# Gate and up of a SwiGLU layer on TensorE: the right operands of the quarter-block products are made step by step between units, and are used from the second and the third pair on

## The chip, the core and the metric

The kernel runs on one core of one Trainium2 chip. The metric is the device time of one execution in microseconds; the time of a kernel is the median over several runs. A profile of one execution shows every instruction of the engines: TensorE (PE, with its weight loads PEld), VectorE (DVE), ScalarE (ACT), GpSimd (POOL) and SyncE (SP), whose queue issues most of the DMA transfers.

## What is computed

One encoder layer on 1024 tokens of width 1024. After the mixers and the first norm, the feed-forward part is the stretch that matters here (cut from the reference):

```
g = jnp.einsum('bsd,df->bsf', h, w_ffn_gate[i])
up = jnp.einsum('bsd,df->bsf', h, w_ffn_up[i])
ffn = jnp.einsum('bsf,fd->bsd', jax.nn.silu(g) * up, w_ffn_down[i])
ple = jnp.einsum('bsr,rd->bsd', p[i], w_ple_proj[i])
ple_gate = jax.nn.sigmoid(jnp.einsum('bsd,de->bse', h, w_ple_gate[i]))
h = _layer_norm(ALPHA * h + ffn + ple_gate * ple, ln2_gain[i], ln2_bias[i])
```

The hidden width is 2816, which is 22 blocks of 128, taken as 11 pairs of blocks.

## The kernel before

**Precision.** Each fp32 operand is split in a high part (an ACT copy to a rounded type, L71) and a low part (a DVE subtraction, L72), both in `split` (L70). A product of two operands is three matmuls, high by high, high by low and low by high: `mm3c` with L783, L784 and L785.

**Gate and up.** Per pair of hidden blocks, gate and up are a 2 by 2 block product in the Strassen-Winograd form with seven products, numbered 1 to 7. The left operands are weights and sums of weights, the right operands (`RIGHT`, one per product) are halves of the transposed hidden state and sums of them, made once ahead of the stage. Each product has two units, m = 0 for gate and m = 1 for up; a unit is 12 matmuls of 128x128 by 128x512. A pair without finer products has the units 1, 1, 2, 2, 6, 6, 7, 7, 5, 5, 4, 4, 3, 3 (`plan`, L1420).

**Finer products.** The products 2 and 4 can themselves be done in seven quarter-block products over gate and up together (`FINE`, L1164). They take 42 matmuls of 128x256 in four parts f0 to f3 (`f_unit`, L1409; `mm_fine`, L1278) in place of 24 of 128x512, and the parts stand between the units of other products: 1, 1, f0, 6, f1, 6, f2, 7, f3, 7 for product 2, and f0, 5, f1, 5, f2, 3, f3, 3 for product 4. They need four further right operands of product 2 and four of product 4, sums of quarter blocks of the hidden state. `fine_right` (L1182) makes them with `make` (L1193): for each of two row blocks three DVE sums of 128x256 (L1197, L1198, L1199), an ACT copy and a DVE subtraction (`split`), all in one scratch tile `fs`. `FROM` (L1165) says from which pair each product is done finely.

**Order.** PE, DVE, ACT, POOL and SP run the program in the order in which the code issues it. All five are queues in order. The loop over the units k (L1779 on) issues the matmuls of unit k, then its `post` (what reads the result out of PSUM), then one of the eight calls of `make` if k is in a list (L1782), and then, in `ahead_g` (L1733), work for later units out of the list `items`. An item is a unit number, a duration that the writer estimated and a function; it is taken while the estimated room of the present unit lasts, up to nine units ahead, or at once if its unit is next.

**Who waits for whom.** The products 1, 6 and 7 of one m are added up in one PSUM bank (`bmm`), and ACT copies the running sum out between them: L1360 after product 1, L1362 after product 6, L1367 after product 7 (`post`, L1344). So the matmuls of product 7 wait for the copy after product 6, and that copy stands on ACT behind whatever splits were issued earlier. The parts of a fine product share banks likewise (`bo` for product 2, `bs` for product 4): f1 waits for the DVE addition that reads f0 out (L1304 in `post_fine`, L1293), f3 for the one after f2. DVE additions that read out products 2, 3 and 5 are L1353, the product of the two halves of 4 is L1376, and L1326 and L1330 finish a pair.

**Down.** Behind the last unit the down product starts with four banks; `dsets` (L1681) names them: the first set is `s` (banks `bs`), then `t` (banks `bmm`; the names were exchanged in L775).

Below, **pair 0** is the first of the 11 pairs, and a unit (6,0) is product 6 with m = 0.

Of the kernel before, what the change touches and what calls it, by code (L numbers as in the profile page):

```python
# [42 lines left out]
def layer(tc, xT, xn, w_first, w_mt, w_rv, w_out, w_pg, w_pe, pT, w_gu, w_dn,  # L43
# [1118 lines left out]

    Q = HF // 2
    FINE = ((1, 5, 2), (6,), (7,), (4, 3))  # L1164
    FROM = {2: 2, 4: 3}  # L1165
    oslots = []
    frights, fsum = {}, []
    TAGS = {0: "t", 1: "o", 2: "mm", 4: "s"}
# [13 lines left out]
    def fine_right(p, places):  # L1182

        R = RIGHT[p]

        def blk(i, j, part):
            return R[:, part, 2 * i:2 * i + 2, j * Q:(j + 1) * Q]

        f = frights[p] = {q: (blk(*ij, 0), blk(*ij, 1)) for q, ij in {1: (0, 0), 2: (1, 0), 3: (1, 1)}.items()}
        f.update(zip((7, 5, 6), places))  # L1190
        f[4] = blk(0, 1, 0), blk(0, 1, 1)

        def make(q, left, right):  # L1193
            x = fsum[3]
            for kt in range(2):
                (lh, ll), (rh, rl) = ([v[:, kt, :].bitcast(F32) for v in side] for side in (left, right))
                dve.tensor_tensor(x, lh, rh, ALU.subtract)  # L1197
                dve.tensor_tensor(x, x, ll, ALU.add)  # L1198
                dve.tensor_tensor(x, x, rl, ALU.subtract)  # L1199
                split(x, *(v[:, kt, :] for v in f[q]))  # L1200

        b = lambda i, j: (blk(i, j, 0), blk(i, j, 1))
        return [lambda: make(7, b(1, 1), b(0, 1)), lambda: make(5, b(0, 1), b(0, 0)),
                lambda: make(6, b(1, 1), f[5]), lambda: make(4, b(1, 0), f[6])]

    stores = []

    class Pair:
# [32 lines left out]
        def prep_fine(self, p, part):  # L1241

            f = self.fine[p]

            def xy():
                return [self.raw[m, p == 4, 1] for m in range(2)]

            def sums():
                x, y = xy()
                dve.tensor_tensor(fsum[0], y[:, :Q], y[:, Q:], ALU.add)  # L1250
                dve.tensor_tensor(fsum[1], fsum[0], x[:, :Q], ALU.subtract)
                dve.tensor_tensor(fsum[2], x[:, :Q], y[:, :Q], ALU.subtract)
# [425 lines left out]

    seq = [(1, 0), (5, 0), (2, 0), (3, 0), (6, 0), (1, 1), (7, 0), (2, 1), (4, 0), (5, 1), (6, 1), (3, 1), (7, 1), (4, 1)]
    which = {(0, 0): 0, (0, 1): 1, (0, 2): 0, (1, 0): 1, (1, 1): 1, (1, 2): 0}  # L1680
    dsets = (("s", "t"), ("o", "mm"))  # L1681
    dunits = []

    def d_units(p, s):
# [81 lines left out]
    with tc.manual_schedule(engines={ET.PE, ET.DVE, ET.Activation, ET.Pool, ET.SP}):  # L1766
# [126 lines left out]
```

## Time and profile before

| what | value |
|---|---|
| median of three runs | 1188.23 us (1187.18 to 1189.41) |
| profiled execution, its own time | 1188.74 us |
| its span, first to last instruction | 1187.0 us |
| PE busy | 1167.6 us, 98% of the span |
| DVE busy | 894.8 us, 75% |
| ACT busy | 578.6 us, 49% |
| gate and up, from the first matmul to the first of down | 539.96 to 968.40 us |

A row of the timeline gives the start from the start of the span, the duration, the engine, the line of the kernel, the operation, the tile written and those read, the shape, and in brackets how long the engine was idle ahead of it and what ended that. A matmul's duration runs to its modelled end, and the next begins before that, so the pace is read from the starts. The table by stretches gives busy time per engine in each stretch, and the granted clock of PE as a share of full speed.

### The profile page before, as it was taken

Reading aid. Unit: us, or ns where it says so; the run is one execution under the profiler, and the core shown is the slowest. Engines: PE = TensorE matmul, PEld = TensorE weight load, DVE = VectorE, ACT = ScalarE, POOL = GpSimd, SP = SyncE. Lnnn points to the kernel's source line nnn. Section 1 sums busy time; section 2 is a strip of 40 time slices with the busy share of each in tenths; the row PEclk is TensorE's granted clock in tenths of the full one; section 3 lists DMA queues with packets and bytes.
Section 4 is the critical chain, followed back from the end, with each engine's and each line's share of the span. In section 5 each row is a group of like instructions: output and inputs, shape, how many; then the busy total and the mean of one; then the engine's idle time right before and its main releaser. Section 6 shows DMA issues by size and latency. Waiting matters only on the chain.

```text
span 1187.0 us, 17890 instructions
## 1 busy us (share of the span) xinstructions
PE 1167.6 (98%) x6374; PEld 981.0 (83%) x6374; DVE 894.8 (75%) x1732; ACT 578.6 (49%) x1177; POOL 119.3 (10%) x181
## 2 busy tenths in 40 slices
PE   9999999999999999999989999999999999999997
PEld 7888888888888888888867888888888888888885
DVE  5565777766759788957878788888888886774677
ACT  5666348676756265123344344433444345552463
POOL 2001011202010130000000000000000011124242
PEclk9999999999999999999989999999999999999999
DMA  7345656555346955665223232322323289999977
GB/s 254 104 160 215 238 171 238 182 168 186 127 172 244 359 179 207 235 219 173 81 70 133 83 113 72 133 98 99 131 74 117 87 241 340 346 236 222 256 166 206
DMA packets 80665, 211.76 MB, mean 178 GB/s; under 512 B 9536, under 2 KB 14784, under 8 KB 80576
## 3 DMA queue, kind: packets, MB, share of 16 engines
q1 hardware_dynamic: 71936, 193.84, 46.2%
q0 software_dynamic: 8640, 16.78, 8.0%
q8 instruction: 50, 0.82, 0.3%
q14 instruction: 39, 0.32, 0.1%
HBM read 139.29 MB, written 62.13 MB: 170 GB/s over the span
## 4 chain that ended last, share of the span: by engine, by line
PE 83%; DVE 9%; ACT 4%; issue 2%; DMA 1%; SPq 0%; DVEq 0%; POOL 0%; ACTq 0%; POOLq 0%
PE bmm L783 7%; PE bmm L784 7%; PE bmm L785 7%; PE bmm L77 5%; PE bmm L79 5%; PE bmm L78 5%; PE bt L783 5%; PE bt L784 5%; PE bt L785 5%; PE bs L783 4%; PE bs L785 4%; PE bs L784 4%; PE bo L783 3%; PE bo L785 3%; PE bo L784 3%
## 5 line engine op out<-in xcount | busy, mean ns | idle before, releaser
L77 PE MATMUL bmm<-H,w 128*128 128x512 f32 x240 | 97.4, 406 | 0.0
L79 PE MATMUL bmm<-H,w 128*128 128x512 f32 x240 | 94.2, 393 | 0.0
L78 PE MATMUL bmm<-H,w 128*128 128x512 f32 x240 | 94.1, 392 | 0.0
L1500 POOL DMA_DIRECT2D h0b<-in_w_dn x24 | 21.6, 900 | 553.6 <-PE bt L785 518.5
L1324 ACT ACTIVATE ev<-ev 128x512 f32<-128x512 f32 x41 | 25.9, 633 | 89.8 <-DVE ev L1353 71.4
L72 DVE TENSOR_TENSOR w<-raw,w 128x512 fp32r<-128x512 f32 (+1 forms) x61 | 39.6, 658 | 18.9 <-ACT w L71 18.7
L77 PEld LDWEIGHTS bmm<-H,w 128*128 128x128 f32 x240 | 45.3, 189 | 9.8 <-ACT H L71 0.7
L79 PEld LDWEIGHTS bmm<-H,w 128*128 128x128 f32 x240 | 45.1, 188 | 9.9
L78 PEld LDWEIGHTS bmm<-H,w 128*128 128x128 f32 x240 | 45.2, 189 | 7.7
L535 ACT ACTIVATE sc<-sc,st 128x385 f32<-128x385 f32 (+1 forms) x64 | 37.1, 584 | 16.8 <-DVE st L533 16.7
L71 ACT ACTIVATE w<-raw 128x512 fp32r<-128x512 f32 (+1 forms) x61 | 35.8, 597 | 17.4 <-PE bo L79 7.6
L531 DVE CUSTOM_DVE_ANT_0 sc<-cst,bs,skb 128x384 f32<-128x384 f32 (+1 forms) x64 | 34.9, 576 | 8.9 <-PE bs L530 7.8
L783 PE MATMUL bmm<-H,u 128*128 128x512 f32 x88 | 35.8, 407 | 3.4 <-ACT ev L1362 3.4
L783 PE MATMUL bmm<-H,w 128*128 128x512 f32 x88 | 35.2, 400 | 3.9 <-ACT ev L1360 2.4
L1326 DVE TENSOR_TENSOR ev<-ev 128x512 f32<-128x512 f32 x41 | 28.4, 692 | 12.8 <-ACT ev L1324 11.9
L784 PE MATMUL bmm<-H,u 128*128 128x512 f32 x88 | 35.5, 403 | 0.0
L785 PE MATMUL bmm<-H,u 128*128 128x512 f32 x88 | 35.3, 401 | 0.0
L1353 DVE TENSOR_TENSOR ev<-ev,bt 128x512 f32<-128x512 f32 x44 | 30.0, 682 | 6.7 <-PE bt L785 6.7
L784 PE MATMUL bmm<-H,w 128*128 128x512 f32 x88 | 35.0, 398 | 0.0
L785 PE MATMUL bmm<-H,w 128*128 128x512 f32 x88 | 35.0, 398 | 0.0
L541 ACT ACTIVATE sc<-sc,st 128x384 f32<-128x384 f32 (+1 forms) x64 | 34.0, 579 | 0.8 <-DVE st L539 0.8
L71 ACT ACTIVATE H<-ln 128x512 fp32r<-128x512 f32 (+1 forms) x34 | 22.9, 677 | 21.5 <-DVE ln L1032 7.2
(786 smaller groups left out, 3845.1 us busy)
## 6 DMA issues: line engine op xcount, KB each, us to landing
ad<-ev SPq DMA_DIRECT2D x33, 512.0 KB, 3.4
pgd<-pro SPq DMA_DIRECT2D x28, 512.0 KB, 2.9
raw<-in_w_gu SPq DMA_DIRECT2D x22, 512.0 KB, 3.6
ln<-in_w_gu SPq DMA_DIRECT2D x22, 512.0 KB, 4.1
raw<-ad SPq DMA_DIRECT2D x40, 256.0 KB, 6.0
ln<-ad SPq DMA_DIRECT2D x37, 256.0 KB, 6.0
H<-in_w_dn SPq DMA_DIRECT2D x33, 256.0 KB, 6.6
wod<-aq SPq DMA_DIRECT2D x15, 512.0 KB, 2.7
```

The source lines that it names most:

```text
L71: act.activation(hi, raw, AF.Copy)
L72: dve.tensor_tensor(lo, raw, hi.bitcast(F32), ALU.subtract)
L77: pe.matmul(o, lh, rh, start=start, stop=False)
L78: pe.matmul(o, lh, rl, start=False, stop=False)
L79: recent[0] = pe.matmul(o, ll, rh, start=False, stop=stop).ins.name
L531: dve.tensor_tensor_reduce(sc[g][:, :nk], cst[:, tc0:tc0 + nk], b[:, :nk], slope(i, g), skb[:, 2 * i + g:2 * i + g + 1], ALU.add, ALU.max, ...
L535: act.activation(sc[g][:, :nk + 1], sc[g][:, :nk + 1], AF.Exp, bias=st_[:, 1, j, g:g + 1], accum_out=st_[:, 2, j, g:g + 1])
L541: behind(act.activation(sc[g][:, :nk], sc[g][:, :nk], AF.Copy, scale=st_[:, 3, j, g:g + 1]))
L783: pe.matmul(o, lh, rh, start=start, stop=False, skip_group_check=True)
L784: pe.matmul(o, lh, rl, start=False, stop=False, skip_group_check=True)
L785: pe.matmul(o, ll, rh, start=False, stop=stop, skip_group_check=True)
L1353: dve.tensor_tensor(get(name), ev[left][:, m, :], right, ALU.add)
```

## The change

Product 2 is done finely from pair 1 on (it was pair 2), product 4 from pair 2 on (it was pair 3). The eight makes are enqueued after the units 2, 4, 7, 9 of pair 0 and 20, 23, 26, 28 of pair 1 (it was 5, 8, 14, 18, 21, 24, 27 and 42, in the old count of units). A make is no longer issued in one piece: it is a list of steps that are put into `items`, one between every two of the items that are there. Six of the eight (all of product 2, and the operands 7 and 5 of product 4) work on both row blocks at once, as 128x(2x256), in a scratch tile `fwide` of their own; the other two work on a row block at a time as before, in `fs`. `last` uses `fsum[1]` in place of that scratch. The first set of banks of the down product is `t`, then `s`.

```
-    FROM = {2: 2, 4: 3}
+    FROM = {2: 1, 4: 2}
...
         def make(q, left, right):
-            x = fsum[3]
-            for kt in range(2):
-                (lh, ll), (rh, rl) = ([v[:, kt, :].bitcast(F32) for v in side] for side in (left, right))
-                dve.tensor_tensor(x, lh, rh, ALU.subtract)
-                dve.tensor_tensor(x, x, ll, ALU.add)
-                dve.tensor_tensor(x, x, rl, ALU.subtract)
-                split(x, *(v[:, kt, :] for v in f[q]))
+            def steps(x, c, us):
+                def rows(pair):
+                    return [v[:, c, :].bitcast(F32) for v in pair]
+
+                return [(us, lambda: dve.tensor_tensor(x, rows(left)[0], rows(right or f[6])[0], ALU.subtract)),
+                        (us, lambda: dve.tensor_tensor(x, x, rows(left)[1], ALU.add)),
+                        (us, lambda: dve.tensor_tensor(x, x, rows(right or f[6])[1], ALU.subtract)),
+                        (us, lambda: split(x, *(v[:, c, :] for v in f[q])))]
+
+            if p == 2 or q in (7, 5):
+                return steps(fwide, slice(0, 2), 0.62)
+            return steps(fsum[3], 0, 0.36) + steps(fsum[3], 1, 0.36)
...
-    dsets = (("s", "t"), ("o", "mm"))
+    dsets = (("t", "s"), ("o", "mm"))
...
+        FINE4 = len(plan(0)) + len(plan(1)) - 2
+        FINES = (2, 4, 7, 9, 20, 23, 26, FINE4)
         ahead_g(-1, 4)
         for k in range(NG):
             gunits[k][1]()
             gunits[k][2]()
-            if k in (5, 8, 14, 18, 21, 24, 27) or k == FINE4:
-                fine.pop(0)()
-                debt[0] += 2.6
+            if k in FINES:
+                if len(fine) == 2:
+                    frights[4][6] = tuple(ct([P, 2, Q], "p", 2, F32R) for _ in range(2))
+                at = max([-1] + [i for i, x in enumerate(items) if x[4:]]) + 1
+                for i, x in enumerate(fine.pop(0)):
+                    at += at > 0
+                    items.insert(at, (items[at][0], 0, *x, True))
+                    at += 1
```

**DVE in pair 0, around the read-out of product 5 (rows into `ev_5333` from `bt`).** Before, a whole make of eight DVE instructions (L1197 to L1199 and the low part, L72, twice) stands between the read-outs of (5,0) and (5,1):

```order
L72 TENSOR_TENSOR u_5324<-raw_5421,u_5324 128x512
L1353 TENSOR_TENSOR ev_5333<-ev_5337,bt_5507 128x512
L1197 TENSOR_TENSOR fs_5338<-h0b_4321 128x256
L1198 TENSOR_TENSOR fs_5338<-fs_5338,h0b_4321 128x256
L1199 TENSOR_TENSOR fs_5338<-fs_5338,h0b_4321 128x256
L72 TENSOR_TENSOR H_5327<-fs_5338,H_5327 128x256
L1197 TENSOR_TENSOR fs_5338<-h0b_4321 128x256
L1198 TENSOR_TENSOR fs_5338<-fs_5338,h0b_4321 128x256
L1199 TENSOR_TENSOR fs_5338<-fs_5338,h0b_4321 128x256
L72 TENSOR_TENSOR H_5327<-fs_5338,H_5327 128x256
L1353 TENSOR_TENSOR ev_5333<-ev_5337,bt_5532 128x512
L1326 TENSOR_TENSOR ev_5333<-ev_5333 128x512
```

Now the same place reads as follows (L1357 is the read-out, L1198 to L1200 are the sums, `p_5331` is the wide scratch; L72 into `w` and `u` are the low parts of left operands):

```order
L72 TENSOR_TENSOR w_5319<-ln_5247,w_5319 128x512
L72 TENSOR_TENSOR H_5327<-p_5331,H_5327 128x512
L1198 TENSOR_TENSOR p_5331<-h0b_4321,H_5327 128x512
L72 TENSOR_TENSOR u_5320<-ln_5249,u_5320 128x512
L1199 TENSOR_TENSOR p_5331<-p_5331,h0b_4321 128x512
L72 TENSOR_TENSOR w_5321<-sums_5325,w_5321 128x512
L1357 TENSOR_TENSOR ev_5333<-ev_5337,bt_5502 128x512
L1200 TENSOR_TENSOR p_5331<-p_5331,H_5327 128x512
L72 TENSOR_TENSOR u_5322<-sums_5326,u_5322 128x512
L72 TENSOR_TENSOR H_5327<-p_5331,H_5327 128x512
L1357 TENSOR_TENSOR ev_5333<-ev_5337,bt_5522 128x512
L1330 TENSOR_TENSOR ev_5333<-ev_5333 128x512
```

Each step of a make now has an instruction of other work behind it, and three instructions stand between the two read-outs where eight stood.

**ACT in pair 1, around the copies after product 6 (L1362 before, L1366 now).** Before, the copy of (6,0) stands behind three splits of left operands, and that of (6,1) behind the two copies of a make (`h0b<-fs`, merged to one row):

```order
L1324 ACTIVATE ev_5337<-ev_5337 128x512
L71 ACTIVATE u_5322<-ln_5484 128x512
L71 ACTIVATE w_5323<-sums_5325 128x512
L71 ACTIVATE u_5324<-sums_5326 128x512
L1362 ACTIVATE ev_5336<-bmm_5620 128x512
L71 ACTIVATE h0b_4321<-fs_5338 128x256 x2
L1362 ACTIVATE ev_5336<-bmm_5644 128x512
```

Now the copy of (6,0) is the row `ev_5336<-bmm_5612`, that of (6,1) the row `ev_5336<-bmm_5634`, in the same pair:

```order
L71 ACTIVATE u_5320<-cst 128x256
L1366 ACTIVATE ev_5336<-bmm_5612 128x512
L71 ACTIVATE u_5322<-ln_5477 128x512
L71 ACTIVATE w_5323<-raw_5436 128x256
L71 ACTIVATE w_5323<-cst 128x256
L1366 ACTIVATE ev_5336<-bmm_5634 128x512
L71 ACTIVATE u_5324<-ln_5497 128x512
```

No copy of a make stands ahead of either; what stands between them are the splits of (7,0) and of f3 of product 2.

**PE at the start of down.** Before, behind the last matmuls of product 3 (into `bt_8679`), the banks `bs` come first:

```order
L785 MATMUL bt_8679<-h_4572,u_5320 128x512
L783 MATMUL bs_8788<-h0a_8666 128x512
L784 MATMUL bs_8788<-h0a_8666 128x512
L785 MATMUL bs_8788<-h0a_8666 128x512
L783 MATMUL bs_8789<-h0a_8666 128x512
```

Now the banks `bmm` come first, and `bs` six matmuls later:

```order
L783 MATMUL bmm_8833<-h0a_8711 128x512
L784 MATMUL bmm_8833<-h0a_8711 128x512
L785 MATMUL bmm_8833<-h0a_8711 128x512
L783 MATMUL bmm_8834<-h0a_8711 128x512
L784 MATMUL bmm_8834<-h0a_8711 128x512
L785 MATMUL bmm_8834<-h0a_8711 128x512
L783 MATMUL bs_8835<-h0a_8711 128x512
```

More of the change, by code (lines that the diff above doesn't have):

```diff
@@ L1193, in make @@
         def make(q, left, right):
-            x = fsum[3]
-            for kt in range(2):
-                (lh, ll), (rh, rl) = ([v[:, kt, :].bitcast(F32) for v in side] for side in (left, right))
-                dve.tensor_tensor(x, lh, rh, ALU.subtract)
-                dve.tensor_tensor(x, x, ll, ALU.add)
-                dve.tensor_tensor(x, x, rl, ALU.subtract)
-                split(x, *(v[:, kt, :] for v in f[q]))
+            def steps(x, c, us):
[8 more added lines that the diff above has]
+            return steps(fsum[3], 0, 0.36) + steps(fsum[3], 1, 0.36)
         b = lambda i, j: (blk(i, j, 0), blk(i, j, 1))
-        return [lambda: make(7, b(1, 1), b(0, 1)), lambda: make(5, b(0, 1), b(0, 0)),
-                lambda: make(6, b(1, 1), f[5]), lambda: make(4, b(1, 0), f[6])]
+        return [make(5, b(0, 1), b(0, 0)), make(7, b(1, 1), b(0, 1)), make(6, b(1, 1), f[5]), make(4, b(1, 0), None)]
     stores = []
@@ L1266, in last @@
                 x, y = xy()
-                dve.tensor_tensor(fsum[3], x[:, Q:], fsum[1], ALU.subtract)
+                dve.tensor_tensor(fsum[1], x[:, Q:], fsum[1], ALU.subtract)
                 put(4, y[:, Q:])
-                put(3, fsum[3], 4)
+                put(3, fsum[1], 4)
                 if p == 4 and self.n + 1 < NP:
@@ L1772, in layer @@
         halves4 = [(fa[:, k, 0], fa[:, k, 1]) for k in range(4)]
-        halves4 += [(ct([P, 2, Q], tag, 2, F32R), ct([P, 2, Q], tag, 2, F32R)) for tag in ("sg", "p")]
-        fine = fine_right(2, halves4[:3]) + fine_right(4, halves4[3:])
+        halves4.append(tuple(ct([P, 2, Q], "sg", 2, F32R) for _ in range(2)))
+        fsum.extend([cst[:, 0:Q], cst[:, Q:2 * Q], cst[:, 2 * Q:3 * Q], ct([P, Q], "fs", 1)])
+        fwide = ct([P, 2, Q], "p", 2)
+        fine, more = fine_right(2, halves4[:3]), fine_right(4, halves4[3:])
+        fine += more
         homes.update((name, a_tile([P, 2, HF], "ev")) for name in ("spare", "s1", "u2", "c11", "u3", "c22"))
-        fsum.extend([cst[:, 0:Q], cst[:, Q:2 * Q], cst[:, 2 * Q:3 * Q], ct([P, Q], "fs", 1)])
-        FINE4 = [k for k, g in enumerate(gunits)].index(sum(len(plan(n)) for n in range(3)) - 2)
+        FINE4 = len(plan(0)) + len(plan(1)) - 2
+        FINES = (2, 4, 7, 9, 20, 23, 26, FINE4)
         ahead_g(-1, 4)
```

## Prediction

> **What bounds the kernel.** I read the busy line of the page first, then who waits on PE, then the table by stretches for the four pairs in which the change works.
>
> ```profile
> span 1187.0 us, 17890 instructions
> PE 1167.6 (98%) x6374; PEld 981.0 (83%) x6374; DVE 894.8 (75%) x1732; ACT 578.6 (49%) x1177; POOL 119.3 (10%) x181
> ```
> ```profile
> PE bmm L783 <- ACT ev L1362: 5.0, 3, 3.2
> PE bmm L783 <- ACT ev L1360: 2.4, 1, 2.4
> ...
> PE bo L783 <- DVE ev L1304: 0.7, 1, 0.7
> PE bs L783 <- DVE ev L1304: 0.7, 1, 0.7
> ```
>
> PE is busy 98% of the span, so time can come only from fewer matmuls or from PE's few waits. Those waits (total, times, longest) are nearly all of gate and up: five matmuls that open a product, held by an ACT copy or a DVE addition out of their bank. The stretches below are pair 0, 1, 2, 3, and pairs 4 to 10 together, each cut at a pair's first matmul; DVE's busy time is the fourth column.
>
> ```profile
> core 0: us, PE busy (x) PEld busy (x) DVE busy (x) ACT busy (x) POOL busy (x), PEclk, DMA share, GB/s
> 539.96:578.63 38.67, 38.39 (x169) 31.49 (x168) 31.29 (x56) 18.66 (x34) 0.00 (x0) 1.00 0.32 108
> 578.63:624.90 46.27, 41.57 (x169) 33.52 (x168) 37.47 (x72) 15.73 (x31) 0.00 (x0) 0.93 0.25 88
> 624.90:667.06 42.16, 39.80 (x187) 33.01 (x186) 34.42 (x66) 17.12 (x33) 0.00 (x0) 0.96 0.33 119
> 667.06:705.45 38.39, 37.67 (x205) 32.54 (x204) 31.26 (x64) 15.55 (x32) 0.00 (x0) 1.00 0.21 73
> 705.45:967.56 262.11, 262.11 (x1429) 227.98 (x1427) 223.94 (x443) 111.41 (x225) 1.97 (x2) 1.00 0.32 114
> ```
>
> Pairs 4 to 10 take 262.11 / 7 = 37.44 us each, PE busy throughout. Pair 1 takes 46.27 for the plainest work. What PE would need there follows from the pace of its starts:
>
> ```profile
> 667.06 0.39 PE L783 MATMUL bmm<-h0a,w 128*128 128x512 f32 x1
> ...
> 672.27 0.39 PE L785 MATMUL bmm<-h0a,u 128*128 128x512 f32 x1
> 672.50 0.28 PE L783 MATMUL bo<-h0b,w 128*128 128x256 f32 x1
> ...
> 674.65 0.40 PE L783 MATMUL bmm<-H,w 128*128 128x512 f32 x1
> ```
>
> From 667.06 to 672.50 run 24 matmuls of 512 columns, 5.44 / 24 = 0.2267 us each, 2.72 a unit; from 672.50 to 674.65 run 18 of 256 columns, 0.119 each. A pair with no fine product needs 14 x 2.72 = 38.08, one with both 37.44, so one fine product saves 0.32. Before, pairs 0 to 3 would need 38.08 + 38.08 + 37.76 + 37.44 = 151.36 and took 38.67 + 46.27 + 42.16 + 38.39 = 165.49: **14.13 us are lost to waits**, 8.19 of them in pair 1 and 4.40 in pair 2.
>
> **Why PE waits there.** The copies after product 6 in pair 1:
>
> ```profile
> 601.00 0.42 DVE L1198 TENSOR_TENSOR fs<-fs,h0b 128x256 f32<-128x256 f32 x1
> 601.46 0.43 DVE L1199 TENSOR_TENSOR fs<-fs,H 128x256 f32<-128x256 f32 x1
> 601.92 0.42 ACT L71 ACTIVATE h0b<-fs 128x256 fp32r<-128x256 f32 x1 [1.87 <-DVE fs L1199]
> 602.24 0.58 ACT L1362 ACTIVATE ev<-bmm 128x512 f32<-128x512 f32 x1
> 602.37 0.43 DVE L72 TENSOR_TENSOR h0b<-fs,h0b 128x256 fp32r<-128x256 f32 x1 [0.48 <-ACT h0b L71]
> 602.87 0.80 PE L783 MATMUL bmm<-H,u 128*128 128x512 f32 x1 [3.15 <-ACT ev L1362]
> ```
>
> ACT cannot copy the bank out (L1362) before it has done the make's copy ahead of it, and that waits for three chained DVE sums. DVE idles 0.48 for ACT as well, since nothing else is queued between a make's sums and its low part. So a make holds DVE for some 2.2 us per row block, and both queues fall behind PE. The long gaps cost a second time:
>
> ```profile
> 594.95:596.67 1.72, 0.17 (x2) 0.01 (x1) 1.54 (x4) 1.66 (x4) 0.00 (x0) 1.00 0.58 145
> 599.56:602.87 3.31, 0.16 (x1) 0.00 (x0) 2.17 (x6) 1.37 (x4) 0.00 (x0) 0.89 0.00 0
> 602.87:608.90 6.03, 6.03 (x14) 4.83 (x15) 4.38 (x8) 3.53 (x8) 0.00 (x0) 0.50 0.47 174
> 632.50:635.01 2.51, 0.15 (x2) 0.00 (x0) 1.85 (x5) 0.95 (x3) 0.00 (x0) 1.00 0.04 15
> 636.30:639.70 3.40, 3.40 (x9) 2.22 (x8) 2.58 (x7) 1.17 (x3) 0.00 (x0) 0.50 0.00 0
> ```
>
> The clock column reads 0.50 for some 6 us behind the gap of 3.31 and for 3.40 behind the gap of 2.51; behind the gap of 1.72 it stays at 1.00. [...]
>
> **The change, part by part.**
>
> *Matmuls.* Two more fine products, 2 x 0.32 = **0.64 us less** for PE, on the path.
>
> *Steps in place of whole makes.* The cost on DVE:
>
> ```profile
> 543.60 0.68 DVE L1078 TENSOR_TENSOR sg<-sg,bs 128x512 f32<-128x512 f32 x1
> 544.20 0.69 DVE L72 TENSOR_TENSOR u<-raw,u 128x512 fp32r<-128x512 f32 x1
> 544.80 0.69 DVE L1080 TENSOR_TENSOR acc<-acc,sg 128x512 f32<-128x512 f32 x1
> 545.40 0.69 DVE L1227 TENSOR_TENSOR sums<-ln 128x512 f32<-128x512 f32 x1
> 546.12 0.69 DVE L1228 TENSOR_TENSOR sums<-sums,raw 128x512 f32<-128x512 f32 x1
> 547.51 0.69 DVE L72 TENSOR_TENSOR w<-sums,w 128x512 fp32r<-128x512 f32 x1 [0.70 <-ACT w L71]
> ...
> 550.84 0.68 DVE L1353 TENSOR_TENSOR ev<-ev,bo 128x512 f32<-128x512 f32 x1
> ```
> ```profile
> L1032 DVE TENSOR_TENSOR ln<-ln,h0b 128x1024 f32<-128x1024 f32 x2 | 2.4, 1222 | 0.0
> ```
>
> Starts are 0.60 apart where the next does not read the last result, and 0.72 (545.40 to 546.12) where it does. A step with other work behind it so costs 0.60. A wide step of 2x256 elements has no row of its own; it lies between 0.42 (256 elements, above) and 1.22 (1024 in one), and I take the 0.60 to 0.69 of 512. A wide make is then 4 x 0.60 = 2.4 us of DVE, where a whole make took 2 x 2.2 = 4.4.
>
> The load by pairs: pair 0 had two makes of eight instructions in its 31.29, at 0.425 these are 6.8; without them it is 24.5, with 16 wide ones at 0.60 it is 34.1 of 38.08. A steady pair with both fine products is 223.94 / 7 = 32.0, so one with product 2 alone lies half way, 28.2; pair 1 adds 8 wide steps and up to 16 narrow ones, 4.8 + 16 x 0.42 = 11.5, in all 39.7 of 37.76, and pair 2 has 32.0 of 37.44. Together 105.8 of 113.3: DVE is 93% full, and pair 1's surplus must slip into pair 2, which items may do.
>
> *Is DVE in time?* In the new order 34 DVE instructions stand between the read-out of (2,0), which nothing new precedes and which started at 550.84, and that of (4,1). At 0.60 the latter starts at 550.84 + 35 x 0.60 = 571.8; two waits for ACT such as the 0.70 above and two chained steps make it 573.5. PE ends (4,1) at 539.96 + 12 x 2.72 = 572.6, so DVE is 0.9 behind, where before it was 5.9 behind:
>
> ```profile
> 578.51 0.68 DVE L1376 TENSOR_TENSOR ev<-ev,bmm 128x512 f32<-128x512 f32 x1
> ```
>
> So the copies after product 6 come in time: each has a whole unit, 2.72, and no make's copy stands ahead of those in pair 1. What is late next is the read-out of f0 in pair 1. Behind the read-out of (3,1), at about 578.5, stand 11 instructions with three more waits for ACT, which end the read-out of f0 at about 588.4; PE wants f1 at 578.04 + 5.44 + 2.16 + 2.74 = 588.4. The margin is nothing, and for f3 it is about 0.1. The nearest row is the same wait in pair 3:
>
> ```profile
> 678.28 0.36 PE L783 MATMUL bo<-H,w 128*128 128x256 f32 x1 [0.71 <-DVE ev L1304]
> ```
>
> I bound what remains between 0 and three such waits of 0.9 (f1 and f3 of pair 1, f1 of pair 2), and take **0.8**. The four pairs then need 38.08 + 37.76 + 37.44 + 37.44 = 150.72 plus 0.8, where they took 165.49: **14.0 us less**, the 0.64 included.
>
> *Banks at the start of down.*
>
> ```profile
> 967.33 0.39 PE L785 MATMUL bt<-h,u 128*128 128x512 f32 x1
> ...
> 967.84 0.74 DVE L1304 TENSOR_TENSOR ev<-ev,bs 128x256 f32<-128x256 f32 x2
> ...
> 968.40 0.47 PE L783 MATMUL bs<-h0a 128*128 128x512 f32 x1 [0.68 <-DVE ev L1304]
> ```
>
> The first matmul could start at 967.56 and started at 968.40, held by the read-out of `bs`. Now `bmm` comes first, whose last copy (L1367) ACT makes units earlier, and `bs` is wanted 6 x 0.227 = 1.36 later, at 968.92, when the read-out has ended (968.58). **0.84 less.**
>
> *Nothing else.* `fsum[1]` in `last` and the other tiles for product 4's operands add no instruction; the weights' loads are issued by the same items. All stages behind shift as a whole, since PE is what they wait for.
>
> **The sum.** Against the profiled execution (1188.74, a span of 1187.0 and 1.7 around it): 1188.74 - 14.0 - 0.84 = 1173.9. That execution lies 0.5 above the median of 1188.23, so the median becomes **1173.4**.
>
> **Rivals.**
>
> A. *One long wait is left.* DVE is 93% full and the margins at f1 and f3 are near zero; if three or four steps run 0.1 longer, or one load comes late, one PE gap of 2.5 stays, with half clock behind it: 2.51 + 3.40 / 2 = 4.2, 1177.6. For it: the table's 39.7 of 37.76 in pair 1. Against: the surplus may slip.
>
> B. *DVE becomes the bound.* If interleaving did not bring 0.72 down to 0.60, the 109 instructions from (2,0)'s read-out to the end of pair 1 would take 13 us more, of which the free 7.5 (113.3 - 105.8) take some: 5.6 of waits and about 2.5 of half clock, 1181.5. The rows at 543.60 to 544.80 speak against it. [...]
>
> C. *The waits are not the makes'.* Then only the matmuls and the banks count, 0.64 + 0.84, 1186.8. Against it: pairs 4 to 10 have 32.0 us of DVE each, no make and no wait.
>
> D. *Slower.* The wide steps read two separate row blocks of a two-part tile. There are 24 on DVE (16 in pair 0, 8 in pair 1); were each 1.3 us or more, above even the 1.22 of 1024 elements, the extra 0.7 x 24 = 16.8 would outweigh the 14.8: 1190.8 with some half clock. It decides from 1.22 up (24 x 0.62). No row hints at that.
>
> **Chances.** The forecast 76%, A 13%, B 6%, C 3%, D 2%. Faster by over 0.2% (2.4 us, about what a measurement of this kernel tells from no change): 95%; within it 3%; slower 2%. The range goes from 1171.5 (nothing left of the 0.8, and 1 us of spread between runs) to 1178.5, which takes in most of A.
>
> **What would show it.** Right: pairs 0 to 3 at about 38.1, 38.2, 37.6 and 37.4 with the clock at 1.00 in all; no PE wait on the copies after products 1 and 6; wide steps of 0.69 with starts 0.60 apart; the product of (4,1) in pair 0 within 1.5 us of PE's end; no wait at the first matmul of down. Wrong: a wait above 2 us or a clock below 1.00 in any of these pairs, a wide step above 0.8, or DVE more than 2.7 behind at the read-out of f0 in pair 1.

## The result, and the profile after

The changed kernel takes **1430.2 us** (median of six runs, 1429.77 to 1432.28) against 1188.38 for the kernel before: a ratio of **1.204 [1.2024, 1.2055]**. The prediction was 1173.4, with 0.95 on faster. It was wrong in sign and by 257 us.

The busy line of the profile after, and the row of PE's granted clock in 40 slices of the span:

```profile
span 1428.7 us, 17911 instructions
PE 1254.4 (88%) x6410; PEld 1009.7 (71%) x6410; DVE 902.3 (63%) x1736; ACT 580.6 (41%) x1179; POOL 118.2 (8%) x181
...
PEclk9999999999999999998998989898998989999999
```

No engine has become the bound. DVE has 902.3 us of work where it had 894.8, and its share has fallen to 63%. PE stands still for longer, and in the slices 19 to 33 its clock dips again and again. The stretches, cut at a pair's first matmul, are pairs 0, 1, 2, 3, and pairs 4 to 10 together:

```profile
core 0: us, PE busy (x) PEld busy (x) DVE busy (x) ACT busy (x) POOL busy (x), PEclk, DMA share, GB/s
540.56:578.64 38.08, 38.08 (x170) 31.53 (x168) 35.23 (x58) 18.68 (x33) 0.00 (x0) 1.00 0.38 136
578.64:617.23 38.59, 37.99 (x187) 31.98 (x186) 33.53 (x62) 15.87 (x31) 0.00 (x0) 1.00 0.27 93
617.23:665.59 48.36, 41.36 (x206) 33.93 (x205) 32.39 (x69) 16.16 (x34) 0.00 (x0) 0.96 0.19 67
665.59:731.98 66.39, 46.96 (x206) 34.96 (x204) 33.02 (x65) 15.95 (x32) 0.00 (x0) 0.92 0.17 60
731.98:1210.22 478.24, 341.45 (x1429) 255.47 (x1428) 232.88 (x452) 113.64 (x228) 1.97 (x2) 0.90 0.18 62
```

Pairs 0 and 1, in which the change works, came out as worked out: 38.08 and 38.59, the clock at 1.00, where they took 38.67 and 46.27. The loss begins in pair 2 and never ends: pairs 4 to 10 take 478.24 / 7 = 68.32 each, where they took 37.44. Their work is that of before: 1429 matmuls, DVE 232.88 us where it had 223.94, ACT 113.64 where it had 111.41. Pairs 2 to 10 need 9 x 37.44 = 336.96 and take 1210.22 - 617.23 = 592.99: **256.0 us lost**, which is the whole miss. Of the 68.32, PE stands still for 19.5 and is busy 48.78 (341.45 / 7), 11.3 more than the 37.44 for the same matmuls. The slowed clock is at most 6.8 of these 11.3, a tenth of 68.32 at a mean clock of 0.90. The rest lies at the breaks: the last matmul ahead of a wait counts with its whole recorded length (0.39 where the pace is 0.227), which no next one overlaps, and the first two behind the wait shown below start 0.34 and 0.39 apart. At a clock of 0.99 (`e10_refill02` below) PE is still busy 241.32 / 6 = 40.2 a pair.

Who waits on PE (total, times, longest). Before, the first rows named read-outs (L1362, L1360); now they name `split`, the high part on ACT (L71) and the low part on DVE (L72) of the left operands:

```profile
PE bmm L783 <- ACT u L71: 48.8, 23, 3.2
PE bmm L783 <- ACT w L71: 32.6, 18, 3.5
PE bmm L785 <- DVE w L72: 23.8, 12, 3.8
```

One such wait, in the timeline of pair 10. The last row is the first matmul of (6,1), the first row the read-out of f1 of product 2:

```profile
1162.47 0.42 DVE L1308 TENSOR_TENSOR ev<-ev,bo 128x256 f32<-128x256 f32 x1 [3.03 <-PE bo L785]
1162.81 0.68 DVE L1231 TENSOR_TENSOR sums<-ln 128x512 f32<-128x512 f32 x1
1163.52 0.69 DVE L1232 TENSOR_TENSOR sums<-sums,raw 128x512 f32<-128x512 f32 x1
1164.31 0.63 ACT L71 ACTIVATE u<-sums 128x512 fp32r<-128x512 f32 x1 [1.95 <-DVE sums L1232]
...
1164.99 0.50 PE L783 MATMUL bmm<-H,u 128*128 128x512 f32 x1 [2.56 <-ACT u L71]
```

Read it as a circle. DVE has stood idle for 3.03 us, because the next thing in its queue is the read-out of a part that PE is still working on. Only behind that read-out stand the two sums (L1231, L1232) that make the left operand of PE's next unit, then ACT's copy of it, and PE has waited 2.56 us for that copy. Every engine waits in turn for another, and none has too much to do. Late loads are not the cause: from 700 to 1210 us no instruction of ACT or DVE waits for a DMA transfer. Before, the same sums stood several units further ahead in the queues, so DVE made them while PE worked.

The order shows it, and showed it before the run. DVE's rows of the changed kernel at the end of pair 2: L1357 and L1330 are the last read-outs of the pair, and `raw_6051` and `raw_6053` are the weights of pair 3, so the two L72 rows are the low parts of the left operands of its first units:

```
L1357 TENSOR_TENSOR ev_5337<-ev_5337,bt_6151 128x512
L1330 TENSOR_TENSOR ev_5337<-ev_5337 128x512
L1334 TENSOR_TENSOR ev_5337<-ev_5337,ev_5333 128x512
L72 TENSOR_TENSOR w_5317<-raw_6051,w_5317 128x512
L72 TENSOR_TENSOR u_5318<-raw_6053,u_5318 128x512
```

In the kernel before, in a pair with both fine products, the same step stands between the parts of product 4, ahead of the read-outs of product 5 (L1353), some seven units earlier in the program (`raw_6936` are the next pair's weights):

```
L1304 TENSOR_TENSOR ev_5333<-ev_5336,bs_7031 128x256
L1304 TENSOR_TENSOR ev_5333<-ev_5333,bs_7031 128x256
L72 TENSOR_TENSOR w_5319<-sums_5326,w_5319 128x512
L72 TENSOR_TENSOR u_5318<-raw_6936,u_5318 128x512
L72 TENSOR_TENSOR u_5320<-raw_6938,u_5320 128x512
L1353 TENSOR_TENSOR ev_5337<-ev_5336,bt_7059 128x512
```

**Theory L.** The loss is one of look-ahead. `ahead_g` (L1733) takes items while the estimated room of the present unit lasts (the next unit's duration, less the read-outs of the unit just issued, less `debt`). At the end it keeps a debt, but no credit: `debt = max(0, -room)` throws away what is left when the next whole item doesn't fit. So a kernel that has fallen short of look-ahead does not build it up again, though every pair has room to spare. Adding up the code's own durations, a pair without fine products has 38.08 - 8.74 (read-outs) - 13.64 (items) = 15.7 us to spare, one with fine product 2 has 11.3, and one with both 5.7. The eight makes cost 20.6 in steps and 20.8 whole. The kernel before had the pairs 0, 1 and 2 to pay them from, 15.7 + 15.7 + 11.3 = 42.7; the changed one has pairs 0 and 1, and the second is already dearer: 15.7 + 11.3 = 27.0. Following the rule of `ahead_g` through all units by arithmetic gives the distance from a unit to the first item not yet issued: 6.2 units on average in pairs 4 to 9 before, and after the change 4.7, 5.2, 3.1 and 2.4 in pairs 0 to 3 and 2.4 for good. (These are sums of the program's estimates and no measurement.)

The rivals. **W**: something in the changed work itself (wide steps, new tiles, banks), and not its place in the order, holds PE. **T**: the shortage is real but passes, since the pairs behind it have room to spare.

### The profile page after: what moved, and what is told of

Read it like the earlier page. It is cut to its first block, busy times and chain, and to the rows that moved or that the text cites. A ratio compares the mean times of both kernels' runs of the same rounds, so it can differ in the third digit from the quotient of the medians.

```text
span 1428.7 us, 17911 instructions
## 1 busy us (share of the span) xinstructions
PE 1254.4 (88%) x6410; PEld 1009.7 (71%) x6410; DVE 902.3 (63%) x1736; ACT 580.6 (41%) x1179; POOL 118.2 (8%) x181
## 3 DMA queue, kind: packets, MB, share of 16 engines
q1 hardware_dynamic: 71936, 193.84, 38.6%
## 4 chain that ended last, share of the span: by engine, by line
PE 81%; DVE 11%; ACT 5%; issue 2%; DMA 0%; DVEq 0%; ACTq 0%; SPq 0%
PE bmm L785 8%; PE bmm L783 8%; PE bmm L784 7%; PE bmm L77 5%; PE bt L785 5%; PE bmm L79 5%; PE bmm L78 5%; PE bt L783 5%; PE bt L784 4%; PE bs L785 3%; PE bs L783 3%; PE bs L784 3%; PE bo L783 3%; PE bo L785 3%; PE bo L784 3%
## 5 line engine op out<-in xcount | busy, mean ns | idle before, releaser
L77 PE MATMUL bmm<-H,w 128*128 128x512 f32 x240 | 97.5, 406 | 0.2 <-ACT H L71 0.2
L79 PE MATMUL bmm<-H,w 128*128 128x512 f32 x240 | 94.1, 392 | 0.0
L78 PE MATMUL bmm<-H,w 128*128 128x512 f32 x240 | 93.9, 391 | 0.0
L783 PE MATMUL bmm<-H,u 128*128 128x512 f32 x92 | 46.0, 500 | 41.5 <-ACT u L71 41.5
L72 DVE TENSOR_TENSOR w<-raw,w 128x512 fp32r<-128x512 f32 (+1 forms) x62 | 40.2, 653 | 52.5 <-ACT w L71 51.9
L1308 DVE TENSOR_TENSOR ev<-ev,bo 128x256 f32<-128x256 f32 x70 | 29.2, 420 | 68.2 <-PE bo L785 67.5
L783 PE MATMUL bmm<-H,w 128*128 128x512 f32 x84 | 39.8, 474 | 30.2 <-ACT w L71 30.2
L783 PEld LDWEIGHTS bmm<-H,u 128*128 128x128 f32 x92 | 22.1, 240 | 48.4 <-ACT u L71 45.0
L1364 ACT ACTIVATE ev<-bmm 128x512 f32<-128x512 f32 x22 | 13.1, 596 | 101.7 <-PE bmm L785 101.7
L77 PEld LDWEIGHTS bmm<-H,w 128*128 128x128 f32 x240 | 45.2, 188 | 10.3 <-ACT H L71 1.1
L1357 DVE TENSOR_TENSOR ev<-ev,bt 128x512 f32<-128x512 f32 x44 | 30.1, 684 | 35.1 <-PE bt L785 35.1
L79 PEld LDWEIGHTS bmm<-H,w 128*128 128x128 f32 x240 | 45.0, 188 | 10.0
L78 PEld LDWEIGHTS bmm<-H,w 128*128 128x128 f32 x240 | 45.2, 188 | 7.8
L1371 ACT ACTIVATE ev<-bmm 128x512 f32<-128x512 f32 x22 | 13.1, 596 | 79.6 <-PE bmm L785 79.6
L785 PE MATMUL bmm<-H,u 128*128 128x512 f32 x92 | 44.1, 479 | 0.9 <-DVE u L72 0.9
L783 PEld LDWEIGHTS bmm<-H,w 128*128 128x128 f32 x84 | 18.7, 223 | 36.4 <-ACT w L71 33.5
L784 PE MATMUL bmm<-H,u 128*128 128x512 f32 x92 | 43.9, 477 | 0.0
L71 ACT ACTIVATE w<-raw 128x512 fp32r<-128x512 f32 (+1 forms) x62 | 36.5, 595 | 15.5 <-PE bo L79 7.6
L785 PE MATMUL bmm<-h0a,w 128*128 128x512 f32 x44 | 21.8, 496 | 22.4 <-DVE w L72 22.4
## 6 DMA issues: line engine op xcount, KB each, us to landing
raw<-ad SPq DMA_DIRECT2D x40, 256.0 KB, 6.0
ln<-ad SPq DMA_DIRECT2D x37, 256.0 KB, 5.9
H<-in_w_dn SPq DMA_DIRECT2D x33, 256.0 KB, 7.5
```

The costliest lines, as they stand in the source:

```text
L71: act.activation(hi, raw, AF.Copy)
L72: dve.tensor_tensor(lo, raw, hi.bitcast(F32), ALU.subtract)
L77: pe.matmul(o, lh, rh, start=start, stop=False)
L78: pe.matmul(o, lh, rl, start=False, stop=False)
L79: recent[0] = pe.matmul(o, ll, rh, start=False, stop=stop).ins.name
L783: pe.matmul(o, lh, rh, start=start, stop=False, skip_group_check=True)
```

## The experiments

All kernels compute the whole result. Times of all pairs, cut at each pair's first matmul (us; pair 10 ends with down, whose first matmul differs by kernel and is left out; each row is one execution):

| kernel | 0 | 1 | 2 | 3 | 4 | 5 | 6 | 7 | 8 | 9 | time |
|---|---|---|---|---|---|---|---|---|---|---|---|
| before | 38.67 | 46.27 | 42.16 | 38.39 | 37.44 | 37.44 | 37.44 | 37.44 | 37.44 | 37.44 | 1188.4 |
| after | 38.08 | 38.59 | 48.36 | 66.39 | 68.73 | 68.22 | 68.18 | 68.39 | 68.14 | 68.30 | 1430.2 |
| e1_cut | 38.53 | 45.02 | 42.35 | 45.75 | 68.30 | 67.70 | 68.60 | 68.42 | 68.24 | 68.24 | 1410.6 |
| e2_refill | 38.08 | 38.60 | 40.19 | 43.05 | 37.46 | 37.44 | 37.45 | 37.43 | 37.44 | 37.43 | 1183.5 |
| e8_refill03 | 38.08 | 38.61 | 46.11 | 39.94 | 37.45 | 37.44 | 37.44 | 37.46 | 37.44 | 37.44 | 1184.6 |
| e10_refill02 | 38.08 | 38.60 | 45.21 | 44.39 | 44.92 | 44.98 | 45.00 | 46.57 | 44.95 | 44.95 | 1248.0 |
| e4_whole | 51.18 | 67.89 | 71.27 | 66.94 | 68.26 | 68.26 | 68.27 | 68.41 | 67.69 | 68.61 | 1496.2 |
| e3_steps | 38.40 | 38.08 | 38.21 | 37.44 | 39.93 | 37.44 | 37.43 | 37.43 | 37.44 | 37.43 | 1177.8 |
| e7_half | 38.41 | 38.60 | 38.25 | 37.44 | 39.97 | 37.45 | 37.45 | 37.46 | 37.44 | 37.46 | 1178.1 |
| e11_carry03 | 38.08 | 38.90 | 39.20 | 39.42 | 38.64 | 38.62 | 38.63 | 38.94 | 38.63 | 38.63 | 1187.3 |
| e6_carry062 | 42.76 | 39.39 | 38.41 | 38.78 | 38.77 | 38.78 | 38.78 | 38.76 | 38.77 | 39.06 | 1191.0 |
| e12_cut_carry | 39.00 | 43.44 | 44.48 | 43.22 | 46.64 | 40.36 | 38.62 | 38.89 | 38.63 | 38.64 | 1211.6 |

Kernels that run the same instructions up to pair 2 (before, `e1_cut`, `e12_cut_carry`) differ there from one execution to the next, in pair 1 between 43.44 and 46.27. So small differences in pairs that hold long waits say nothing.

**The old kernel with its look-ahead cut in one pair** (`e1_cut`). Nothing of the change is in it; during pair 3 alone (units 44 to 61) it may look three units ahead in place of nine.

```
-            ahead_g(k, k + 1 + min(9, 4 + k))
+            ahead_g(k, k + 1 + (3 if 44 <= k < 62 else min(9, 4 + k)))
```

> The kernel before, with nothing of the change, but in pair 3 alone the planner may take items at most 3 units ahead in place of 9; from pair 4 on the limit is 9 again. Theory L (the order of the code lost its look-ahead in pair 2 and never wins it back, and a pair with a look-ahead of 2 to 3 units takes 68 us): pairs 4 to 10 take 68.2 each although the limit is lifted, pair 3 between 48 and 67, in all 7 x 30.8 + 10 to 29 more than before: 1414 to 1433. Rival W (the fine products' new operands, where they lie or how they are made, slow PE in every later pair): none of them is in this kernel, so 1188, at most 1190 with a hitch in pair 3. Rival T (the look-ahead grows again once the limit is lifted): pair 3 alone loses, 1198 to 1217.

Measured: 1410.63 (one run). Its stretches for pair 3, pair 4 and pair 10:

```profile
666.13:711.88 45.75, 40.91 (x206) 33.20 (x204) 28.26 (x57) 14.30 (x29) 0.00 (x0) 0.96 0.18 61
711.88:780.18 68.30, 48.57 (x205) 36.34 (x204) 33.02 (x65) 15.95 (x32) 0.00 (x0) 0.90 0.16 58
1121.38:1189.62 68.24, 48.50 (x205) 36.26 (x203) 34.90 (x68) 17.92 (x36) 1.97 (x2) 0.90 0.28 89
```

The cut ends with pair 3, and pair 10, seven pairs later, still takes 68.24, the figure of the changed kernel (68.32), with its busy time and its clock. So L holds and T falls, and nothing of W's is needed for pairs of 68. By the arithmetic of theory L this kernel, too, looks 2.4 units ahead from pair 4 on. The time lies 3 us under the range that L gave.

**The changed kernel, with its look-ahead filled up again** (`e2_refill`): 0.62 us more room for each of the units 30 to 49, in pairs 2 and 3. The makes, their places and the fine products stay as changed.

```
         room = units[k + 1] - gunits[k][4] - debt[0] if k >= 0 else 100.0
+        room += 0.62 if 30 <= k < 50 else 0.0
```

> The changed kernel, with one more number: the planner's room is 0.62 larger at each of the units 30 to 49 (pair 2 and the first units of pair 3), so that it takes about one more item per unit there. Everything else of the change is in. Theory L: the look-ahead is back by pair 3 and stays, pairs 3 to 10 take 37.4 each, and the kernel lands near the prediction, 1173 to 1178 (the extra items load DVE in pair 2). Rival W: the later pairs stay at 68, 1420 to 1430.

Measured: 1183.5 (1182.11 to 1184.66), 0.996 [0.9946, 0.9975]. Pair 3, and pairs 4 to 10 together:

```profile
657.17:700.22 43.05, 39.02 (x206) 33.63 (x204) 32.18 (x64) 15.78 (x31) 0.00 (x0) 0.96 0.29 92
700.22:962.30 262.08, 262.08 (x1429) 227.93 (x1428) 223.85 (x443) 111.46 (x225) 1.98 (x2) 1.00 0.33 114
```
```profile
671.70 0.58 PE L783 MATMUL bo<-H,u 128*128 128x256 f32 x1 [4.03 <-DVE ev L1308]
```

One line takes 247 us off the changed kernel, and pairs 4 to 10 are back at 262.08 (262.11 before), with everything of the change in it. W falls. The mechanism is L's; the size was a miss, some 5 us above the range. The refill puts so many items ahead of a read-out (L1308) that PE waits 4.03 for it, with a dip of the clock behind (0.96 over pair 3).

**A smaller refill over fewer units, and a smaller one yet** (`e8_refill03`: 0.3 for units 30 to 47; `e10_refill02`: 0.2 for units 30 to 65). For both, the line of `e2_refill` with these numbers.

```
+        room += 0.3 if 30 <= k < 48 else 0.0
```
```
+        room += 0.2 if 30 <= k < 66 else 0.0
```

> The changed kernel with 0.3 more room at the units 30 to 47, less per unit than the refill of 0.62. By the planner's numbers the look-ahead falls to 2 once in pair 2, is 4 and more in pair 3 and stays. Theory L: pair 2 loses some 5 where its look-ahead is short, no 4 us wait in pair 3, 1176 to 1182. If the refill's own load on DVE is what cost e2_refill its 8 us, pair 3 is at 37.4 to 38.5 here.

> The changed kernel with 0.2 more room at the units 30 to 65. By the planner's numbers this refills half: the look-ahead stays at a third level for good, 3.7 units on average and 2 at the least, between the 2.4 of the changed kernel and the 6.2 of before. Theory L with the time set by the look-ahead: pairs 4 to 10 all alike and between 37.4 and 68, I estimate 45 to 60, in all 1240 to 1350. If any refill cures: 1175 to 1185. If only the full look-ahead counts: above 1400.

Measured: `e8_refill03` 1184.57 (1183.51 to 1185.92), 0.9964 [0.995, 0.9978], and `e10_refill02` 1248.03 (one run). The first has the steady 37.44 from pair 4 on, and loses 8.7 in pair 2, before the refill has worked, and 2.5 in pair 3: 3 us above its range. The second lies in its range and settles at a level of its own; the stretch is pairs 4 to 9:

```profile
707.87:979.24 271.37, 241.32 (x1226) 195.87 (x1225) 195.24 (x385) 95.83 (x192) 0.00 (x0) 0.99 0.25 88
```

271.37 / 6 = 45.2 a pair, at a clock of 0.99. So there is no single good and bad state: where the refill stops, the kernel stays. By the arithmetic this kernel looks 3.7 units ahead on average, against 2.4 and 6.2.

**The makes in one piece at the new places** (`e4_whole`), the rest as changed.

```
-                at = max([-1] + [i for i, x in enumerate(items) if x[4:]]) + 1
-                for i, x in enumerate(fine.pop(0)):
-                    at += at > 0
-                    items.insert(at, (items[at][0], 0, *x, True))
-                    at += 1
+                for x in fine.pop(0):
+                    x[1]()
+                debt[0] += 2.6
```

> The changed kernel (fine products from pair 1 and 2 on, new places, new banks), but each make is issued whole at its place, with the old debt of 2.6 us. Theory L: the debt takes the room of the planner earlier than the steps did, the look-ahead is 2 to 3 units from pair 1 on, so pairs 1 and 2 are slow as well: 1450 to 1490. If the slow pairs come from the steps being queued as items: 1175 to 1190.

Measured: 1496.17 (one run). Pair 0 and pair 1:

```profile
540.78:591.96 51.18, 43.47 (x170) 33.51 (x168) 34.40 (x54) 18.07 (x32) 0.00 (x0) 0.90 0.27 96
591.96:659.85 67.89, 48.39 (x188) 35.73 (x188) 39.40 (x73) 17.25 (x34) 0.00 (x0) 0.82 0.18 64
```

The time is 6 us above the range of L, which has the pairs right. Whole makes at these places lose the look-ahead two pairs earlier, and the kernel sits at the same 68.3. So the steps are not what does the harm; where the makes are paid from is.

**The steps alone** (`e3_steps`): the kernel before with its makes in steps and the wide scratch, at the old places (after units 5, 8, 14, 18, 21, 24, 27 and the second last unit of pair 2), with the old first pairs and the old banks.

```
-    FROM = {2: 1, 4: 2}
+    FROM = {2: 2, 4: 3}
...
-        FINES = (2, 4, 7, 9, 20, 23, 26, FINE4)
+        FINES = (5, 8, 14, 18, 21, 24, 27, FINE4)
```

> The kernel before with the makes cut in single steps (wide for six of the eight), but at the old places and with the fine products from the old pairs on, and the old banks for down. Theory L together with the prediction's reading of the waits: the look-ahead stays at 4 units and more from pair 4 on, the waits of pairs 1 and 2 go, 1175 to 1180. If the steps themselves cost the look-ahead for good: above 1380. If the whole makes were not what PE waited for: 1186 to 1190.

Measured: 1177.75 (1177.34 to 1178.86), **0.9914 [0.9899, 0.9929]**. Pair 1, and pair 4 with the longer of the two waits that are left in it (the other is 0.31):

```profile
578.40:616.48 38.08, 38.08 (x169) 31.53 (x168) 31.45 (x52) 14.94 (x27) 0.00 (x0) 1.00 0.34 111
692.13:732.06 39.93, 38.19 (x205) 32.47 (x204) 34.02 (x68) 16.78 (x34) 0.00 (x0) 1.00 0.27 99
```
```profile
704.91 0.36 PE L783 MATMUL bo<-H,u 128*128 128x256 f32 x1 [1.43 <-DVE ev L1308]
```

Pair 1 takes exactly the 14 x 2.72 = 38.08 that its matmuls need: the waits of before were the makes', and steps remove them. Pairs 0 to 4 lose 38.40 + 38.08 + 38.21 + 37.44 + 39.93 - (38.08 + 38.08 + 37.76 + 37.44 + 37.44) = 3.3 us, where before lost 14.1 in pairs 0 to 3.

**Product 2 finely from pair 1 on, product 4 not before pair 3** (`e7_half`); banks and steps as changed.

```
-    FROM = {2: 1, 4: 2}
+    FROM = {2: 1, 4: 3}
...
-        FINE4 = len(plan(0)) + len(plan(1)) - 2
-        FINES = (2, 4, 7, 9, 20, 23, 26, FINE4)
+        FINE4 = len(plan(0)) + len(plan(1)) + len(plan(2)) - 2
+        FINES = (2, 4, 7, 9, 21, 26, 30, FINE4)
```

> The changed kernel with product 4 done finely from pair 3 on as before (its makes at the units 21, 26, 30 and 44), product 2 from pair 1 on. By the planner's own numbers the look-ahead then is 4 units and more from pair 4 on. Theory L: no slow pairs, 1174 to 1180. If using the fine products earlier is what makes the later pairs slow, whatever the look-ahead: about 1300 or more.

Measured: 1178.07 (1177.41 to 1178.46), 0.9905 [0.9888, 0.9922]. With product 4 one pair later, and its four makes moved with it, the whole loss is gone (pairs 2 and 3: 38.25 and 37.44). The kernel moves both, so it doesn't tell the first pair from the places; by the arithmetic it is the pair that decides: with the new places and the old first pairs the distance settles at 6.2 units, with product 4 alone from pair 2 on at 3.7 or at 2.4, according to where its makes stand. Those two were not tried. Product 2's earlier pair does no harm, and brings nothing that the times show beside `e3_steps`: the 0.32 of one fine product is less than what the pairs differ by.

**The banks alone** (`e5_banks`): the kernel before, with the change's order of banks at down.

```
-    dsets = (("s", "t"), ("o", "mm"))
+    dsets = (("t", "s"), ("o", "mm"))
```

> The kernel before with the new order of banks at the start of down alone. The prediction's reading (the first matmul of down waits 0.84 for the read-out of its bank): 0.8 to 0.9 less, 1187.4, no wait at the first matmul of down. If the wait only moves to the next bank: 1188.2.

Measured: 1187.37 (1185.79 to 1187.86, ten runs) against 1188.65, 0.9984 [0.9975, 0.9994]: 1.28 less by the medians, 0.7 to 3.0 by the interval, with the expected 0.84 near its low end. In its trace the first matmul of down starts 0.23 behind the last of product 3 (966.71 and 966.94), and the first one into `bs` follows at 968.30 without a wait.

**Keeping the room that was thrown away** (`e11_carry03` and `e6_carry062`): the changed kernel, with a credit of up to 0.3 or 0.62 us carried from unit to unit.

```
-        debt[0] = max(0.0, -room)
+        debt[0] = max(-0.3, -room)
```

> The changed kernel, but what the planner leaves of a unit's room is carried to the next unit, up to 0.3, where it was dropped. Theory L with its reason for the lasting loss (room that is too small for the next whole item is thrown away, so a look-ahead once lost is not won back): the look-ahead is at 5 to 7 units from pair 3 on by itself, pairs 3 to 10 take 37.4, in all 1173 to 1180. If the loss lasts for another reason: above 1240.

> The same with up to 0.62 carried, so 8 units of look-ahead in pair 1 already. Theory L: no slow pairs; as DVE is fuller in pairs 0 and 1, one or two waits of 1 to 3 us there, 1174 to 1181. If the loss lasts for another reason: above 1240.

Measured: 1187.27 (1186.35 to 1187.83), 0.9987 [0.9978, 0.9996], and 1191.02 (1189.86 to 1192.04), 1.0021 [1.0011, 1.003]. Of the waits for a split one of 0.33 us is left (in pair 2 of `e11_carry03`), so the look-ahead is cured; but both are a miss, 7 and 10 us above their ranges. In `e11_carry03` every pair from pair 1 on has a wait at f1 of product 2, here that of pair 8, with DVE's queue ahead of it:

```profile
860.42 0.68 DVE L1235 TENSOR_TENSOR sums<-raw,sums 128x512 f32<-128x512 f32 x1
861.25 0.69 DVE L72 TENSOR_TENSOR u<-ln,u 128x512 fp32r<-128x512 f32 x1
861.86 0.87 DVE L1308 TENSOR_TENSOR ev<-ev,bo 128x256 f32<-128x256 f32 x2
...
862.78 0.39 PE L783 MATMUL bo<-H,u 128*128 128x256 f32 x1 [0.91 <-DVE ev L1308]
```

The read-out of f0 (L1308) stands behind sums and splits for later units, and f1 waits for it. That is 0.9 of the 1.2 us by which each pair is over 37.44, ten times over. With 0.62 the pairs are at 38.77, and pair 0 loses 4.7 more, most of it at one wait: the copy after product 6 stands on ACT behind three splits, the first of which waits 2.80 us for DVE:

```profile
562.71 0.68 PE L783 MATMUL bmm<-H,u 128*128 128x512 f32 x1 [2.68 <-ACT ev L1366]
```

So too much look-ahead costs too, on the other side: it puts work for later ahead of read-outs that are wanted now. By the arithmetic these two look 7.2 and 7.9 units ahead.

**Cut and credit together** (`e12_cut_carry`): the kernel of `e1_cut`, with the credit of 0.3 from unit 44 on, where the cut begins.

```
-        debt[0] = max(0.0, -room)
+        debt[0] = max(-0.3 if k >= 44 else 0.0, -room)
```

> The kernel before with the cut to 3 units in pair 3, as in e1_cut, and with 0.3 of room carried from pair 3 on. Theory L: pair 3 at about 46 as there, pair 4 at 40 to 60 while the look-ahead returns, pairs 5 to 10 at 37.4: 1198 to 1218 where e1_cut took 1410. If carrying does not help: 1390 to 1410.

Measured: 1211.62 (one run). Pairs 3, 4 and 5, then 6 to 9 together:

```profile
666.80:710.02 43.22, 38.92 (x205) 32.38 (x204) 27.65 (x56) 13.67 (x28) 0.00 (x0) 1.00 0.19 65
710.02:756.66 46.64, 39.78 (x205) 32.27 (x204) 34.24 (x69) 16.95 (x34) 0.00 (x0) 1.00 0.25 85
756.66:797.02 40.36, 38.51 (x206) 32.45 (x204) 35.32 (x70) 17.00 (x37) 0.00 (x0) 1.00 0.27 98
797.02:951.80 154.78, 150.85 (x818) 129.76 (x816) 128.61 (x256) 63.06 (x129) 0.00 (x0) 1.00 0.29 103
```

The same cut, but now pair 5 is nearly done with it and pairs 6 to 9 take 38.7 each, as in `e11_carry03`, where 37.4 was expected. It is the thrown-away room that keeps the look-ahead low for good. With it kept, theory T would have been right.

**Steps and banks together, the best kernel looked for** (`e13_steps_banks`): `e3_steps` with the order of banks of `e5_banks`.

> The kernel before with the makes in steps at the old places (those of the kernel with steps alone, which took 1177.75), first used from the old pairs, and with the new order of banks at down (which alone was worth 1.3). If the two parts touch different stretches they add up: 1176.4 to 1176.9, pairs 0 to 10 as with steps alone (38.4, 38.1, 38.2, 37.4, 39.9, then 37.4 each), the down product without a wait at its start. If the last pair's read-outs bound the start of down, nothing comes of the banks: 1177.7.

Measured: 1177.71 (1176.77 to 1177.99), 0.9908 [0.9892, 0.9925], no different from `e3_steps`. The range for two parts that add up was missed, and the reason that was given for 1177.7 doesn't hold either, since the wait at the start of down is gone. In the profiled executions the banks do their work: from pair 10's first matmul to the first of down it takes 957.69 - 920.25 = 37.44, where `e3_steps` takes 957.49 - 919.23 = 38.26. But its pair 0 takes 38.84 where that of `e3_steps` takes 38.40, with a wait of 0.5 on L1366 that the other has not, and it begins 0.49 later. Whether these belong to the change of banks or to the one execution was not tried. Both kernels beat the one before by 0.9%.

## Why the prediction was wrong, step by step

- *What the makes cost, and what steps save.* Right. Pairs 0 and 1 took 38.08 and 38.59, where 38.08 and 37.76 + 0.8 were worked out, the clock at 1.00, no wait on the copies after products 1 and 6. `e3_steps` shows it without the rest: 1177.75.
- *Wide steps.* Right: 0.69 each, and 0.60 to the next start where other work stands behind. So rivals B and D had no ground. A wide step and what stands behind it:

```profile
571.74 0.69 DVE L1199 TENSOR_TENSOR p<-p,h0b 128x512 f32<-128x512 f32 x1
572.34 0.68 DVE L72 TENSOR_TENSOR u<-raw,u 128x512 fp32r<-128x512 f32 x1
```

- *What is left at f1.* Right in place and size: 0.8 was taken, and pair 1 took 38.59 - 37.76 = 0.83 more than its matmuls.
- *Banks.* Right: the first matmul of down follows the last of product 3 by 0.22.

```profile
1210.00 0.39 PE L785 MATMUL bt<-h,u 128*128 128x512 f32 x1
1210.22 0.39 PE L783 MATMUL bmm<-h0a 128*128 128x512 f32 x1
```

- *"Pair 1's surplus must slip into pair 2, which items may do."* **This step failed.** It weighed how much DVE has to do (105.8 of 113.3 us in pairs 0 to 2) and took the rest for free. DVE did have the time: pairs 0 to 2 kept it busy for 35.23 + 33.53 + 32.39 = 101.2, less than was worked out, and in pair 2 that is 32.39 of 48.36. What was spent was not DVE's time but the distance between a left operand's making and its use. Items that slip are the left operands of coming units, and each unit by which they slip brings them nearer to the matmul that waits for them.
- *"All stages behind shift as a whole, since PE is what they wait for."* **This failed with it**, and made the size. It treated pairs 3 to 10 as fixed at 37.44, because they were so before. Their 37.44 hung on a look-ahead that they inherited from pair 2 and pass on unchanged; `e1_cut` takes it away without any of the change, and 37.44 becomes 68.3 for seven pairs.
- *Rivals.* A (one long wait left, 1177.6) counted one wait where each pair got a dozen. D, the slower one, sought the price in the steps' durations. None asked what the order of later pairs would be, though that could be read from the order of the changed kernel without a run.
- *What would show it wrong.* The list named a clock below 1.00 or a wait above 2 us in pairs 0 to 3, and that is where it showed, in pairs 2 and 3 (clocks of 0.96 and 0.92).

## What to carry to other kernels

Where a program issues work for later units by a rule that spends estimated room, look-ahead is a stock and not a flow: work put in ahead draws it down, and if the rule forgets unused room, it stays down in every iteration that follows. Before costing such an insertion, read from the order how many units ahead the operands of the *steady* iterations stand, before and after; a steady pace of before is no property of the iteration, if that distance has moved. Both ends cost: here some 2.4 units ahead gave 68.3 us a pair, 6.2 gave 37.44, and 7.2 to 7.9 gave 38.6 to 38.8, since read-outs then stand behind work for later.

## What the runs showed of the hardware that was not expected

The price of a wait isn't fixed by its length. In `e10_refill02` the pairs 3 to 10 each have one wait of 1.70 us (1.69 once) ahead of the first matmul of a unit, for an ACT split. Behind six of the eight the granted clock stays at 1.00; behind two it drops. One of each:

```profile
820.20 0.50 PE L783 MATMUL bmm<-H,u 128*128 128x512 f32 x1 [1.70 <-ACT u L71]
...
865.18 0.50 PE L783 MATMUL bmm<-H,u 128*128 128x512 f32 x1 [1.70 <-ACT u L71]
```

The pair of the second wait is 46.57 long, that of the first 45.00. The clock records tell the two waits apart. From 540 us to the end of gate and up, the clock changes 4 times in the trace of the kernel before and 62 times in that of the changed one, in each only at moments that lie whole multiples of 3.41 us apart. Cut into such steps, counted from the fall of the clock at 866.58, the two places of `e10_refill02` read:

```profile
818.79:822.21 3.42, 1.93 (x7) 1.32 (x8) 2.57 (x6) 1.15 (x2) 0.00 (x0) 1.00 0.50 152
822.21:825.62 3.41, 1.98 (x9) 1.19 (x9) 0.87 (x2) 2.01 (x5) 0.00 (x0) 1.00 0.00 0
863.17:866.58 3.41, 1.64 (x8) 0.91 (x7) 2.38 (x6) 1.15 (x2) 0.00 (x0) 1.00 0.61 187
866.58:869.99 3.41, 3.41 (x9) 2.30 (x7) 0.49 (x2) 0.00 (x0) 0.00 (x0) 0.50 0.02 5
```

The first wait begins at 818.50, so the end of a step at 818.79 cuts it in two; the second lies whole in one step, PE is busy for only 1.64 of that step, and the next one runs at 0.50. Five of the eight waits are cut so, and none of them costs clock; three lie whole in a step, and two of these are followed by a half clock (the third has PE busy 1.72 in its step). The traces of the kernels before and after hold 283 such steps at full clock. Of the 248 in which PE stands still for less than 1.6 us by its recorded matmuls, none is followed by a step at 0.50; of the 31 with more than 1.94, all are; of the four between, two. So what the lower clock goes with in these traces is that PE stands still for about half of one step or more, and equal waits cost differently by where they fall on the steps.

In the changed kernel the wait of 2.56 in pair 10 is followed by a lower clock:

```profile
1164.99:1169.68 4.69, 4.69 (x12) 3.42 (x13) 1.01 (x2) 0.26 (x1) 0.00 (x0) 0.64 0.00 0
```

A dozen matmuls at full speed would take 12 x 0.227 = 2.72, and these take 4.69, so the wait costs some 2 us more than its own length.
